# The second FFN projection by quarters with seven products

## The chip, the cores and the metric

The kernel runs on one core of a Trainium2 chip. The metric is the device time of one execution in microseconds, as a median of several runs. Three runs of the kernel before took 1961.64, 1966.53 and 1968.09 us, so its median is 1966.53 us.

Engines go by the names of the profile: PE multiplies matrices (PEld is its loading of the stationary operand), DVE and ACT work on tiles, POOL is a further engine that here does small vector work, and SP issues the transfers from device memory (HBM).

## What is computed

Two blocks run one after the other over 512 tokens of width 1024, each with two layers. The first block is left alone by the change. Each of the two layers of the second block ends in a feed-forward part (FFN), of which this is the core:

```python
def conv_ffn(x, w_up, conv_w, conv_b, w_down):
    a, g = jnp.split(x @ w_up, 2, axis=-1)
    g = lax.conv_general_dilated(g, conv_w[:, None, :].astype(g.dtype), window_strides=(1,),
                                 padding=((CONV_W - 1, 0),), dimension_numbers=('NWC', 'WIO', 'NWC'),
                                 feature_group_count=D_FF) + conv_b
    return (jax.nn.gelu(g) * a) @ w_down

    # in the layer: y = conv_ffn(...); x = layer_norm(alpha * x + y, ln_g[l, 1], ln_b[l, 1])
```

The hidden width `D_FF` is 2816, that is 22 chunks of 128. The change is about the last product, `(...) @ w_down`: 512 tokens x 2816 times 2816 x 1024.

## The kernel before

**Split numbers.** Every fp32 operand of a large product is kept as a pair (hi, lo): ACT casts the raw tile to fp32r for hi (L226 for weights), and DVE subtracts hi from the raw tile for lo (L227). One product step is then three matmuls into the same PSUM bank: hi by hi, hi by lo, lo by hi. `dsteps` (L231 to L233) has tokens as the stationary side and weights of 512 columns moving. `fsteps` (L1060 to L1062) has weights as the stationary side and 512 tokens moving.

**Weight slots.** `load_w` has SP load a raw tile (128x512, 256 KB, four buffers), takes the next of the slots in `wslots` in turn, and splits into it. Six slots are always there. `more_w` adds 7 in the FFN, so 13 in all. A slot is free again when PE has done the last matmul that reads it.

**The FFN** (`ffn`, called once a layer, the first at about 890 us, the second at about 1575 us) goes over the 22 chunks in three parts of 8, 7 and 7. Within a part, groups of at most four chunks take two passes of `fsteps`, the gate pass and the linear pass: a chunk is 8 steps of 3 matmuls, then its evacuation. `ev_g` does bias and scale on ACT (L1490), two shifted multiply-adds on DVE (L1491, L1492) and the GELU on ACT. `ev_a` multiplies by the linear half on DVE (L1497) and splits the result into `act` on ACT and DVE (L1499, L1500). Then comes the down stage of the part: for both halves of 512 output columns and the four tiles of 128 tokens, one step for each chunk of the part, and a DVE instruction that adds the bank to the running sum `z` (L1532). In the last part that is followed by the layer norm of the token tile (L1142 to L1152, with two small instructions on POOL, L281 and L282). After the first layer's FFN, the first projection of the next mixer (`start_odd`, 312 columns) is woven in between the last down steps.

**Order.** Each engine carries out its own queue in order. The queues are laid out ahead by a recording layer that interleaves the instructions by its own estimate, so they don't stand in the order of the code. Within one queue, an instruction that waits holds up all behind it.

The tile `yT` holds the mixer's output for the out projection ahead of the FFN and isn't used in it.

## Time and profile before

| | |
|---|---|
| median of three runs | 1966.53 us (1961.64 to 1968.09) |
| profiled execution, device time | 1962.12 us |
| its span, first to last instruction | 1960.3 us |
| PE busy in the span | 97% (1899.6 us, 10240 matmuls) |
| DVE, ACT, POOL busy | 60%, 40%, 10% |
| mean granted clock of PE | 0.991 of full speed |
| HBM traffic over the span | 106 GB/s |

The rows that are read from the trace stand in a section of their own below. A row gives line, engine, operation, output<-input by the program's names, and shape. In a list by time the columns are start and duration in us, and in brackets the idle time of the engine just ahead of the instruction with what ended it. Matmuls overlap: the duration of one (0.39 us) is its way through the array, and the distance between the starts of two is what it costs.

### The profile page before, as it was taken

What the parts mean: (1) busy time and instruction counts of PE and PEld (TensorE: products, weight loads), DVE (VectorE), ACT (ScalarE), POOL (GpSimd) and SP (SyncE); (2) the same over time, 40 slices, a digit from 0 to 9 for tenths busy, and PEclk for the clock granted to TensorE, in tenths of its full rate; (3) what the DMA queues carried; (4) which work ended last, traced back from release to release, by engine and by line L of the source; (5) the groups of instructions that cost most, each with busy time, mean ns of one, the idle gap of its engine ahead of it and who ended that gap; (6) DMA issues with size and microseconds to landing.
All of it is one profiled execution on the core that took longest, in us unless ns stands there. A gap on an engine that the chain in (4) does not pass through costs nothing.

```text
span 1960.3 us, 29102 instructions
## 1 busy us (share of the span) xinstructions
PE 1899.6 (97%) x10240; PEld 1540.1 (79%) x10240; DVE 1167.4 (60%) x2892; ACT 782.5 (40%) x1760; POOL 203.2 (10%) x316
## 2 busy tenths in 40 slices
PE   7999899999999999999999999999999999999998
PEld 4777687877888888768888888888778788888886
DVE  5698887475774235687434444645776774344445
ACT  2432454432553345444323333234665543233330
POOL 3011102012101000110000000101441200000001
PEclk9999999989999999999999999999999999999999
DMA  8535425135234233404322332352113042223321
GB/s 275 170 91 179 130 86 160 58 109 155 65 103 143 65 94 118 162 1 128 94 86 86 108 98 85 112 168 86 42 41 130 24 129 92 86 87 107 99 86 69
DMA packets 132872, 206.18 MB, mean 105 GB/s; under 512 B 20866, under 2 KB 57076, under 8 KB 132725
## 3 DMA queue, kind: packets, MB, share of 16 engines
q1 hardware_dynamic: 132724, 204.31, 33.9%
q8 instruction: 81, 1.33, 0.3%
q14 instruction: 67, 0.54, 0.1%
HBM read 194.62 MB, written 14.09 MB: 106 GB/s over the span
## 4 chain that ended last, share of the span: by engine, by line
PE 72%; DVE 6%; POOL 2%; DMA 1%; issue 1%; ACT 1%; POOLq 0%; DVEq 0%; ACTq 0%
PE mm L1060 11%; PE mm L1062 11%; PE mm L1061 11%; PE mm L231 9%; PE mm L233 9%; PE mm L232 8%; PE t L1095 1%; PE t L274 1%; PE o L1854 1%; PE o L1662 1%; PE mm L1924 1%; DVE w L227 1%; DVE z L1152 1%; DMA raw<-in_ffn_w_up_dram 1%; PE o L939 1%
## 5 line engine op out<-in xcount | busy, mean ns | idle before, releaser
L226 ACT CAST w<-raw 128x512 fp32r<-128x512 f32 (+4 forms) x568 | 321.8, 581 | 401.2 <-PE mm L233 172.1
L227 DVE TENSOR_TENSOR w<-raw,w 128x512 fp32r<-128x512 f32 (+4 forms) x560 | 348.4, 643 | 174.4 <-ACT w L226 171.7
L1060 PE MATMUL mm<-hT,w 128*128 128x512 f32 x920 | 367.0, 399 | 0.0
L1062 PE MATMUL mm<-hT,w 128*128 128x512 f32 x920 | 362.4, 394 | 0.0
L1061 PE MATMUL mm<-hT,w 128*128 128x512 f32 x920 | 361.6, 393 | 0.0
L231 PE MATMUL mm<-w,hT 128*128 128x512 f32 (+3 forms) x704 | 278.2, 396 | 1.2 <-ACT hT L243 1.2
L233 PE MATMUL mm<-w,hT 128*128 128x512 f32 (+3 forms) x704 | 263.2, 374 | 0.0
L232 PE MATMUL mm<-w,hT 128*128 128x512 f32 (+3 forms) x704 | 261.5, 371 | 0.5 <-DVE w L227 0.5
L1062 PEld LDWEIGHTS mm<-hT,w 128*128 128x128 f32 x920 | 172.6, 188 | 40.0 <-DVE w L227 0.8
L1060 PEld LDWEIGHTS mm<-hT,w 128*128 128x128 f32 x920 | 172.9, 188 | 39.7 <-ACT w L226 1.1
L1061 PEld LDWEIGHTS mm<-hT,w 128*128 128x128 f32 x920 | 172.9, 188 | 36.1
L231 PEld LDWEIGHTS mm<-w,hT 128*128 128x128 f32 x704 | 139.8, 199 | 30.4 <-issue 6.9
L233 PEld LDWEIGHTS mm<-w,hT 128*128 128x128 f32 x704 | 139.8, 199 | 20.7 <-issue 1.1
L232 PEld LDWEIGHTS mm<-w,hT 128*128 128x128 f32 x704 | 140.1, 199 | 16.8 <-issue 1.8
L231 PE MATMUL mm<-w,act 128*128 128x512 f32 x352 | 139.0, 395 | 0.0
L232 PE MATMUL mm<-w,act 128*128 128x512 f32 x352 | 138.3, 393 | 0.0
L233 PE MATMUL mm<-w,act 128*128 128x512 f32 x352 | 138.2, 393 | 0.0
L1532 DVE SCALAR_TENSOR_TENSOR z<-z,mm 128x512 f32<-128x512 f32 x48 | 33.0, 687 | 109.8 <-PE mm L233 109.8
L1491 DVE SCALAR_TENSOR_TENSOR g<-mm,cw,g 128x511 f32<-128x511 f32 x44 | 33.0, 749 | 100.2 <-ACT g L1490 100.2
L281 POOL TENSOR_SCALAR rp<-mv 128x1 f32<-128x1 f32 x16 | 9.8, 614 | 775.9 <-DVE mv L1146 774.9
L1090 ACT ACTIVATE E<-E,nm 128x128 f32<-128x128 f32 (+3 forms) x128 | 71.6, 560 | 45.5 <-DVE nm L1089 42.8
L1497 DVE TENSOR_TENSOR ge<-ge,mm 128x512 f32<-128x512 f32 x44 | 30.2, 686 | 83.3 <-PE mm L1062 83.3
(433 smaller groups left out, 3060.0 us busy)
## 6 DMA issues: line engine op xcount, KB each, us to landing
raw<-in_ffn_w_up_dram SPq DMA_DIRECT2D x128, 256.0 KB, 2.9
rawm<-in_w_mod_dram SPq DMA_DIRECT2D x96, 256.0 KB, 3.1
raw<-in_ffn_w_down_dram SPq DMA_DIRECT2D x88, 256.0 KB, 3.0
raw<-in_w_in_dram SPq DMA_DIRECT2D x80, 256.0 KB, 2.8
raw<-in_ev_w_in_dram SPq DMA_DIRECT2D x48, 256.0 KB, 3.1
raw<-in_ffn_w_up_dram SPq DMA_DIRECT2D x64, 192.0 KB, 2.4
raw<-in_w_out_dram SPq DMA_DIRECT2D x32, 256.0 KB, 3.0
raw<-in_w_in_dram SPq DMA_DIRECT2D x32, 128.0 KB, 3.5
```

What stands on the lines that cost most here:

```text
L226: SC.copy(hi, r)
L227: (eng or V).tensor_tensor(lo, r, hi.bitcast(F32), op=OP.subtract)
L231: PE.matmul(ps, hi, w[:, 0, w0:w0 + n], start=first, stop=False)
L232: PE.matmul(ps, hi, w[:, 1, w0:w0 + n], start=False, stop=False)
L233: PE.matmul(ps, lo, w[:, 0, w0:w0 + n], start=False, stop=last)
L1060: PE.matmul(ps, wh, hi, start=k == ks[0], stop=False)
L1061: PE.matmul(ps, wh, lo, start=False, stop=False)
L1062: PE.matmul(ps, wl, hi, start=False, stop=k == ks[-1])
L1090: SC.activation(E, E, AF.Exp, scale=scale, bias=nm, accum_out=den)
L1491: V.scalar_tensor_tensor(g0[:, 1:], ps[:, :S - 1], cw[:, 1, c:c + 1], g0[:, 1:], op0=OP.mult, op1=OP.add)
L1497: V.tensor_tensor(ge[j], ge[j], ps, op=OP.mult)
L1532: V.scalar_tensor_tensor(hs, hs, R2 if part == 0 else 1.0, ps, op0=OP.mult, op1=OP.add)
```

## The change

The parts of the FFN are now 8, 8 and 6 chunks. In the first two (`quart`), the down product is done by quarters: tokens are cut into halves of 256, output columns into halves of 512, and the chunks of the part are taken in four pairs (2p, 2p+1). The 2x2 by 2x2 product of such blocks, eight products otherwise, is done with seven of sums and differences (Strassen's scheme in Winograd's form). The last part is as before, with six chunks.

`quarters` makes the token side of a pair, after the second chunk's `ev_a`: four sums of 256 columns (DVE) and splits of three tiles of 512 and one of 256 columns (a cast on ACT and a subtraction on DVE for each). `down_quart` makes the weight side. `operand` splits four tiles `bq` into four weight slots; three of the seven sets are loaded plainly by SP, and the four others are running sums: a DMA that POOL issues adds the next quarter of the weights to the tile `bq` in place, after both halves of the split have read it. The sum `y` is used for the 1st, 3rd, 5th and 7th product, the sum `x` for the 4th and 6th, with at least one other product between two uses of one sum. `product` runs one of the seven: 4 pairs x 2 token tiles x 3 matmuls = 24 matmuls of 512 columns. Banks are added to `z` after each product's turn on them (`take`, L1537), 14 times a part.

`more_w` adds 3 slots in place of 7, so 9 in all. `g0` has three buffers in place of two, and the small tile `cwr` of the convolution weights takes one of them. Of the operand tiles of the token side, some lie in `yT`.

```diff
-        more_w(f"wf{l}", 7, fst, "left")
-        cwr = fp.tile([88, 128], F32, name="cwr")
+        more_w(f"wf{l}", 3, fst, "left")
+        cwr = fp.tile([128, S], F32, name="g0", bufs=3)[:88, :128]
...
-        for part, nch in enumerate((8, 7, 7)):
-            act = [fp.tile([128, 2, S], F32R, name="act", bufs=10) for _ in range(nch)]
+        for part, (nch, quart) in enumerate(((8, True), (8, True), (6, False))):
...
+            def quarters(p, r0, r1):
+                lh, rh = slice(0, 256), slice(256, 512)
+                k1, m, u2, v = ops[p]
+                u = fp.tile([128, S], F32, name="g0", bufs=3)
+                V.tensor_tensor(u[:, lh], r0[:, lh], r0[:, rh], op=OP.subtract)
+                V.tensor_tensor(r0[:, rh], r1[:, rh], r0[:, rh], op=OP.subtract)
+                split(m[:, 0], m[:, 1], r0)
+                split(k1[:, 0], k1[:, 1], r1)
+                V.scalar_tensor_tensor(u[:, rh], r0[:, rh], -1.0, r0[:, lh], op0=OP.mult, op1=OP.subtract)
+                split(u2[:, 0], u2[:, 1], u)
+                V.scalar_tensor_tensor(r1[:, lh], u[:, rh], -1.0, r1[:, lh], op0=OP.mult, op1=OP.subtract)
+                split(v[:, 0], v[:, 1], r1[:, lh])
...
+                def operand(name, b=None, then=None):
+                    ws = []
+                    for p in range(npair):
+                        if b:
+                            bufs[name, p] = fp.tile([128, 512], F32, name="bq", bufs=8)
+                            nc.sync.dma_start(bufs[name, p], src[b](p))
+                    for p in range(npair):
+                        wturn[0] = (wturn[0] + 1) % len(wslots)
+                        px, nx = wslots[wturn[0]]
+                        w = px.tile([128, 2, 512], F32R, tag="w", name="w", bufs=nx)
+                        split(w[:, 0], w[:, 1], bufs[name, p])
+                        ws.append(w)
+                        if then:
+                            GP.dma_start(bufs[name, p], src[then](p), accum_op=OP.add)
+                    return ws
...
+                def take(n, t, sub, ps, mul=1.0):
+                    hs = z[t][:, 512 * n:512 * n + 512]
+                    V.scalar_tensor_tensor(hs, hs, mul, ps, op0=OP.mult, op1=OP.subtract if sub else OP.add)
...
+                o1 = operand("y", (0, 0), (0, 1))
+                o2 = operand("s", (1, 0))
+                product(0, o1, X, True, False, False, lambda r, ps: take(0, r, False, ps, first))
+                o5 = operand("y", None, (1, 1))
+                product(1, o2, W, True, True, False, lambda r, ps: take(0, r, False, ps))
+                o3 = operand("x", (1, 1), (0, 1))
+                product(4, o5, Y, True, False, True, lambda r, ps: take(1, 2 + r, True, ps, first))
+                o6 = operand("y", None, (1, 0))
+                product(2, o3, Y, False, True, True, lambda r, ps: take(1, r, True, ps, first))
+                o7 = operand("x")
+                product(5, o6, X, False, False, True, lambda r, ps: take(1, r, True, ps))
+                o4 = operand("y")
+                product(6, o7, X, False, False, True, lambda r, ps: take(1, 2 + r, True, ps))
+                product(3, o4, X, False, True, True, lambda r, ps: take(0, 2 + r, False, ps, first))
```

How the queues stand now, at two places. First DVE, at the hand-over from the last linear pass of part one to its down stage, first layer. Before, the row `ge<-ge,mm` is `ev_a` and `z<-z,mm` the first use of the down product:

```order
L1497 TENSOR_TENSOR ge<-ge,mm 128x512
L227 TENSOR_TENSOR w<-raw,w 128x512
L1500 TENSOR_TENSOR act<-ge,act 128x512
L227 TENSOR_TENSOR w<-raw,w 128x512 x4
L1497 TENSOR_TENSOR ge<-ge,mm 128x512
```

And now (L1496, L1497, L1500 and L1502 are the four sums of `quarters`, L244 is the subtraction of a split, `act<-ge` the tiles m and k1, `act<-g` the tile u2, `w<-bq` weights of `operand`):

```order
L1582 TENSOR_TENSOR ge<-ge,mm 128x512
L1496 TENSOR_TENSOR g_9878<-ge 128x256
L244 TENSOR_TENSOR w<-bq,w 128x512 x7
L1582 TENSOR_TENSOR ge<-ge,mm 128x512
L244 TENSOR_TENSOR w<-bq,w 128x512
L1497 TENSOR_TENSOR ge<-ge 128x256
L244 TENSOR_TENSOR w<-bq,w 128x512
L1500 SCALAR_TENSOR_TENSOR g_9878<-ge 128x256
L244 TENSOR_TENSOR act<-ge,act 128x512 x2
L244 TENSOR_TENSOR act<-g_9878,act 128x512
L1502 SCALAR_TENSOR_TENSOR ge<-g_9878,ge 128x256
L1537 SCALAR_TENSOR_TENSOR z_8186<-z_8186,o 128x512
```

Nine weight subtractions stand ahead of the last pair's tiles, two of them (the 8th and 9th, of the third product) behind the last `ev_a`.

Second, ACT at the same place, before:

```order
L226 CAST w<-raw 128x512
L1499 CAST act<-ge 128x512
L226 CAST w<-raw 128x512 x5
L1499 CAST act<-ge 128x512
L226 CAST w<-raw 128x512 x18
L1490 ACTIVATE g_10213<-mm,cw 128x512
```

and now:

```order
L243 CAST w<-bq 128x512
L1579 ACTIVATE ge<-g_9715 128x512
L243 CAST act<-ge 128x512 x2
L243 CAST act<-g_9813 128x512
L243 CAST yT<-ge 128x256
L243 CAST w<-bq 128x512 x9
L243 CAST act<-ge 128x512 x2
L243 CAST act<-g_9878 128x512
L243 CAST w<-bq 128x512 x2
```

The casts of the last pair's tiles m and k1 (`act<-ge 128x512 x2`) stand behind nine weight casts, of which the last two read a `bq` that POOL's DMA has added to.

## Rows read from the trace of the kernel before

**Rows 1.** The page's head and busy times (us, share of the span, instructions).

```profile
span 1960.3 us, 29102 instructions
PE 1899.6 (97%) x10240; PEld 1540.1 (79%) x10240; DVE 1167.4 (60%) x2892; ACT 782.5 (40%) x1760; POOL 203.2 (10%) x316
```

**Rows 2.** Busy time by stretch, the two FFNs: length, engines, clock, DMA share, GB/s.

```profile
896.00:1262.00 366.00, 364.02 (x1667) 300.16 (x1668) 177.90 (x280) 126.16 (x214) 4.80 (x6) 1.00 0.34 102
1580.00:1952.40 372.40, 368.35 (x1688) 302.46 (x1686) 181.70 (x285) 124.03 (x210) 6.51 (x8) 1.00 0.31 97
```

**Rows 3.** The down product's first matmul of each step: ns min/median/max, first and last start.

```profile
L231 PE MATMUL mm<-w,act x352: 388/395/477, 989.3 to 1951.5; 128*128 128x512 f32 x176
```

**Rows 4.** By time, PE: first matmul of a down stage, and the first behind it.

```profile
989.26 0.40 PE L231 MATMUL mm<-w,act 128*128 128x512 f32 x1
...
1033.73 0.39 PE L1060 MATMUL mm<-hT,w 128*128 128x512 f32 x1
```

**Rows 5.** Busy time by stretch: PE, PEld, DVE, ACT, POOL; two passes, then a down stage.

```profile
944.50:989.20 44.70, 44.70 (x195) 36.29 (x194) 21.25 (x33) 17.80 (x29) 0.00 (x0) 1.00 0.32 98
989.20:1033.70 44.50, 44.50 (x193) 36.05 (x193) 16.66 (x25) 10.06 (x17) 0.00 (x0) 1.00 0.31 98
```

**Rows 6.** Groups of instructions by form: count | busy us, mean ns | idle before, releasers.

```profile
L226 ACT CAST w<-raw 128x512 fp32r<-128x512 f32 x424 | 257.2, 620 | 342.3 <-PE mm L233 158.3 <-PE mm L1062 61.0 <-DMA raw<-in_ffn_w_up_dram 41.5
L227 DVE TENSOR_TENSOR w<-raw,w 128x512 fp32r<-128x512 f32 x416 | 280.9, 695 | 132.6 <-ACT w L226 130.4
L227 DVE TENSOR_TENSOR w<-raw,w 128x256 fp32r<-128x256 f32 x48 | 19.8, 432 | 23.9 <-ACT w L226 23.5
L1532 DVE SCALAR_TENSOR_TENSOR z<-z,mm 128x512 f32<-128x512 f32 x48 | 33.0, 687 | 109.8 <-PE mm L233 109.8
L1491 DVE SCALAR_TENSOR_TENSOR g<-mm,cw,g 128x511 f32<-128x511 f32 x44 | 33.0, 749 | 100.2 <-ACT g L1490 100.2
L1497 DVE TENSOR_TENSOR ge<-ge,mm 128x512 f32<-128x512 f32 x44 | 30.2, 686 | 83.3 <-PE mm L1062 83.3
```

**Rows 7.** By time, the kernel's end: DVE's layer norm of a token tile, PE's last matmul.

```profile
1947.47 0.69 DVE L1532 SCALAR_TENSOR_TENSOR z<-z,mm 128x512 f32<-128x512 f32 x1
1948.19 0.69 DVE L1142 BATCH_NORM_STATS2 st<-z 128x6 f32<-128x512 f32 x1
1948.92 0.21 DVE L1146 BATCH_NORM_AGGREGATE mv<-st 128x2 f32<-128x12 f32 x1
1949.16 1.42 DVE L1151 SCALAR_TENSOR_TENSOR z<-z,mv,lng 128x512 f32<-128x512 f32 x2
1951.02 1.42 DVE L1152 SCALAR_TENSOR_TENSOR z<-z,rstd,lnb 128x512 f32<-128x512 f32 x2 [0.44 <-POOL rstd L282]
1951.92 0.39 PE L233 MATMUL mm<-w,act 128*128 128x512 f32 x1
1952.35 0.69 DVE L1532 SCALAR_TENSOR_TENSOR z<-z,mm 128x512 f32<-128x512 f32 x1
```

**Rows 8.** By time, PE's waits ahead of FFN passes and after the first FFN.

```profile
907.66 0.39 PE L1517 MATMUL mm<-hT,w 128*128 128x256 f32 x1 [1.98 <-ACT w L226]
1269.04 0.41 PE L232 MATMUL mm<-w,hT 128*128 128x312 f32 x1 [0.54 <-DVE w L227]
1279.21 1.29 PE L274 MATMUL t<-con,z 128*128 128x128 f32 x8 [0.36 <-DVE z L1152]
1592.70 0.39 PE L1517 MATMUL mm<-hT,w 128*128 128x256 f32 x1 [2.65 <-ACT w L226]
```

**Rows 9.** DMA issues: count, KB each, median us from issue to landing.

```profile
raw<-in_ffn_w_down_dram SPq DMA_DIRECT2D x88, 256.0 KB, 3.0
TA<-skA SPq DMA_DIRECT2D x4, 256.0 KB, 5.2
skA<-rd SPq DMA_DIRECT2D x8, 320.0 KB, 6.4
```

**Rows 10.** The page's DMA queues: packets, MB, share of 16 engines.

```profile
q1 hardware_dynamic: 132724, 204.31, 33.9%
```

More of the change, by code (lines that the diff above doesn't have):

```diff
@@ L1488, in ev_g @@
                     c = c0 + q0 + j
-                    g0 = fp.tile([128, S], F32, name="g0", bufs=2)
+                    g0 = fp.tile([128, S], F32, name="g0", bufs=3)
                     SC.activation(g0, ps, AF.Identity, scale=cw[:, 2, c:c + 1], bias=cw[:, 3, c:c + 1])
@@ L1497, in ev_a @@
                     V.tensor_tensor(ge[j], ge[j], ps, op=OP.mult)
+                    if quart:
+                        if j % 2:
+                            quarters((q0 + j) // 2, ge[j - 1], ge[j])
+                        return
                     d = act[q0 + j]
@@ L1549, in finish @@
                     save_x(t, z[t])
-            if part == 2:
-                lg = rows(1)
+            if quart:
+                down_quart()
+                c0 += nch
+                continue
+            lg = rows(1)
             w = [{k: load_w(down, 128 * (c0 + k), 512 * n, 512) for k in range(nch)} for n in range(2)]
```

33 lines of the change are left out of this document (added).

## The prediction

> **What bounds the kernel now.** I read the busy times first: PE is busy for 97% of the span, no other engine for more than 60% [rows 1]. A busy PE need not be PE at its limit, so next I read the stretches of the two FFNs: PE busy 364.0 of 366.0 us and 368.4 of 372.4 us at a granted clock of 1.00, that is 2.4 GHz, with DVE and ACT busy for under half [rows 2]. PE's only long waits there stand at the start of each FFN (1.98 and 2.65 us), with two short ones after the first [rows 8]. Within a down stage nothing is waited for: 44.50 of 44.50 us [rows 5]. So there the number of matmuls times their distance sets the time. The duration in a row (395 ns, [rows 3]) is not that distance; the starts are: the first down stage runs from 989.26 to 1033.73 us, 44.47 us for 8 chunks x 8 outputs x 3 = 192 matmuls [rows 4], **0.2316 us each**. A step of three is 0.695 us, and a pass of one chunk (8 steps) or one of the seven products (also 8 steps) 5.56 us.
>
> **The term that pays.** A part of 8 chunks took 192 matmuls and takes 7 x 24 = 168. Two parts in two layers: 4 x 24 = 96 fewer, of the same form. 96 x 0.2316 = **22.2 us**. The cut into 8, 8, 6 for 8, 7, 7 moves chunks between parts and costs no matmul. This is the ceiling, were nothing on DVE, ACT or in the DMAs late.
>
> **Load of DVE and ACT.** In a down stage there are now 28 weight subtractions at 0.695 us and 14 adds to z at 0.687 us [rows 6]: 19.5 + 9.6 = 29.1 us on DVE of 7 x 5.56 = 38.9 us, 75% where it was 16.7 of 44.5 [rows 5]. ACT has 28 casts at 0.62 us, 17.4 us. In a pass over four chunks and its gate pass (44.5 us), DVE has 16 subtractions (11.1 us), four evacuations of 0.749 x 2 + 0.686 us (8.7 us), and for each of two pairs four sums and a half split at 0.432 us (the 256-column row) and three splits at 0.695 us, 4.2 us a pair: 28.3 us, 64%. Neither engine becomes the bound by its sum. What remains is lateness at single places.
>
> **Hand-over into the down stage, four times.** Set zero at the first matmul of the first product. From the end of PE's slot to a waiting engine's start takes 0.2 us (PE's last matmul starts at 1951.92, its slot ends 0.23 us later, DVE starts at 1952.35, [rows 7]). The slot for the 7th weight that stands ahead of the last `ev_a` comes free at -0.5, its cast ends at 0.12 and its subtraction at 0.85. Then DVE's queue goes: `ev_a` to 1.54, the third product's first weight to 2.23, a sum to 2.66, its second weight to 3.35 (slot free at 1.6, cast done at 2.2), a sum to 3.78, the low half of m to 4.47. PE needs m of the last pair at step 6 of the first product, 4.17, and the low half for its third matmul, 4.63. So the margin is **0.16 us**: about nothing, and I charge 0.4 us each, **1.6 us**. Later in the stage each set is split about one product ahead of its use, since its slots come free when the product two ahead ends; banks and adds to z likewise have half a product or more.
>
> **The adding DMAs.** Their work is new: the trace has no DMA that POOL issues (all data goes by one queue, [rows 10]) and none that adds. The tightest one is the second `y` tile: split by -3.36, and its sum is read at 1.6, at the latest at 2.2 if m is not to be late. So issue to landing may take **5.6 us**. A plain load of that size takes 3.0 us; another source of the same size shows 5.2, and the slowest median shown is 6.4 [rows 9]. I take it near 3.0, as the nearest in size and source, with room for the second read: no wait. At 6.4 it costs 0.8 us x 4 = 3.4 us. It can't be below zero, since nothing waits for DMA there today. The later sums have 7 us or more from split to use. The Trainium skill ("DMA: Bandwidth & Descriptors", Anatomy of one DMA — SWDGE path) gives for a DMA issued by GpSimd 2.0 us plus bytes by 436 GB/s, an estimate of 2.6 us for 256 KB, with no price for an add; by it there is no wait either. No row here shows it. Queued behind them on POOL is only the layer norm at the FFN's end. SP now loads 12 tiles a part where it loaded 16, and POOL adds 16; the DMA engines are 33.9% busy [rows 10]. In SP's queue, the loads for the next part's sums wait for tiles that the 6th and 7th product free, about 28 us into the stage, and raw loads for the next part's fifth and later weights wait behind them. Those are used from 3 us after the stage's end at 38.9: some 10 us of cover for loads of 3.0 us, so nothing; without the cover it is one load, 3 us a part.
>
> **Nine slots in place of thirteen.** Between two passes, weight k of the next pass can only be split when step k of the last chunk is done, and is needed one pass (5.56 us) later. Release, cast and subtraction take 0.2 + 0.62 + 0.695 = 1.5 us. But DVE must do 8 subtractions (5.6 us) and two gate evacuations (3.0 us), or a pair's 4.2 us with two `ev_a`, in about 11 us. Walking the queue as it now stands, the last weights come some 0.7 us (gate to linear) and 1.0 us (linear to gate) ahead of need. There are 9 such hand-overs a layer; I charge 0.1 us each, **1.8 us**, with bounds 0 and 0.6 us each.
>
> **The two ends.** In the last down stage a token tile takes PE 6 chunks x 3 x 0.2316 = 4.17 us, before 7 x 3 x 0.2316 = 4.86. DVE's chain for a tile runs from 1947.47 to 1952.44 with hardly a gap, 4.9 us [rows 7]: so far it just kept up. Now it falls back 0.73 us a tile, three times: **2.2 us** at the kernel's end, nothing hides it. After the first FFN the same chain feeds transposes that other matmuls cover; waits of 0.54 and 0.36 us stand there [rows 8], and with the weights of `start_odd` now waiting for slots I add **0.5 us** (0 to 2).
>
> **The starts.** The waits of 1.98 and 2.65 us name weight casts that stand ahead of the last token casts in ACT's queue. Now five of the first weights are split earlier. I count **1 us** back (bounds: 4.6 us back, 3 us lost).
>
> **The sum.** 22.2 - 1.6 - 1.8 - 2.2 - 0.5 + 1.0 = **17 us**. Against the profiled execution (1962.1 us) that is 1945. This execution is near the fastest of the three runs; the mean of the four times is 1964.6 us. From there: **1947.5 us**.
>
> **Rivals.**
> 1. *The starts free up and the walk holds:* 22.2 - 2.2 + 4 = 24 us, 1938 to 1941. For it: the margins above are positive. Against: the waits at the start may be of the transfers themselves.
> 2. *Nine slots bind:* at 0.5 to 0.6 us for each of 18 hand-overs, 9 to 11 us in place of 1.8: gain 8 to 10 us, 1955 to 1957. For it: margins under 1 us on a chain of three engines, and DVE's queue is in order. Against: DVE is below 75%, and a late weight makes up time in the next pass.
> 3. *Adding DMAs land late.* Each us past 5.6 holds ACT's queue at the 9th cast, behind it m, and with it PE, in each of four stages. At 7 to 9 us from issue to landing it costs 6 to 14 us: 1953 to 1961. **From 9.9 us on the gain of 17 is gone, and at 12 us the kernel is slower: 1973 us.** For it: four such DMAs follow each other from one engine in 3 us. Against: no row of this size is above 5.2 us. The Trainium skill ("SBUF — State Buffer", SBUF: two separate sides) warns that a DMA issued by GpSimd starves while DVE runs a 2-port operation (3100 for 620 ns there); by its section Who interferes with whom, tensor_tensor, which the subtractions here are, has no such mode. No row here shows either.
>
> **How the numbers follow.** The forecast (1942 to 1953) gets 0.64, rival 1 0.08, rival 2 0.10, rival 3 up to 1961 us 0.09, and beyond that 0.09. The range for 8 in 10 takes the forecast and rivals 1 and 2: 1938 to 1958. A measurement of this kernel can tell about 0.3%, 5.9 us. Faster by more are the forecast, rivals 1 and 2 and two thirds of the partly late DMAs, 0.88, of which I take 0.06 off to within 0.3%, since late DMAs and short slots can add up: 0.82. Within 0.3% then are 0.03 + 0.01 + 0.06 = 0.10, slower 0.08.
>
> **What would show it.** PE with 10144 matmuls, 96 fewer than 10240 [rows 1]. Down stages of some 39 us. A wait of PE for DVE's m (L244) or ACT's cast within the first product speaks for the hand-over term; if ACT's `w<-bq` rows there show idle time that a DMA ended, it is rival 3, and the DMA rows give its landing. PE waits for L227 at passes' starts speak for rival 2. At the end, DVE's last chain starts 2 us or more after PE's last matmul. Wrong would be all of this if the distance of matmuls in the new stage isn't 0.23 us.

## The result and the profile after

The changed kernel took a median of 1939.75 us in four runs (1935.72 to 1946.16) where the kernel before took 1965.76 (1961.64 to 1968.09). The ratio is 0.9882, 95% interval 0.9843 to 0.992: some 23 us faster. The prediction was 1947.5 us with a range from 1938 to 1958 us, so the direction and the range held, while the gain is larger than the 17 us of the forecast. The median lies in the band of rival 1 (1938 to 1941 us), not in that of the forecast (1942 to 1953 us); a later repeat of the same kernel took 1942.69 us, so the time alone does not tell the two apart, and the stages below have to.

The profiled execution of the changed kernel took 1936.26 us. First the page's head, the busy times and the queue that is new (packets, MB, share of 16 engines), to be read against [rows 1] and [rows 10]:

```profile
span 1934.5 us, 29305 instructions
PE 1874.2 (97%) x10144; PEld 1518.6 (79%) x10144; DVE 1251.6 (65%) x3060; ACT 828.1 (43%) x1840; POOL 260.1 (13%) x380
q0 software_dynamic: 9216, 16.78, 5.2%
```

PE has its 96 matmuls less, and DVE is at 65%. Next, busy time by stretch. The columns are the stretch, its length, busy time of PE, PEld, DVE, ACT and POOL with counts, granted clock, DMA share and GB/s. The stretches are the first FFN's half stage (its first gate pass, in halves of 256 tokens), the four Strassen stages, the second FFN's half stage (fourth row), and the last down stage to the kernel's end:

```profile
893.58:918.49 24.91, 24.32 (x203) 23.92 (x201) 12.80 (x21) 9.23 (x15) 1.68 (x2) 1.00 0.59 191
985.00:1024.30 39.30, 39.30 (x170) 31.44 (x168) 30.20 (x50) 19.15 (x33) 10.55 (x12) 1.00 0.91 209
1112.42:1151.28 38.86, 38.86 (x170) 31.53 (x169) 30.34 (x50) 19.14 (x33) 10.57 (x12) 1.00 0.76 158
1563.49:1591.71 28.22, 25.90 (x211) 24.90 (x209) 17.29 (x29) 11.26 (x19) 1.45 (x2) 1.00 0.56 189
1658.30:1697.41 39.11, 39.04 (x170) 31.45 (x168) 30.33 (x50) 19.11 (x33) 10.55 (x12) 1.00 0.91 211
1785.57:1824.56 38.99, 38.99 (x170) 31.52 (x168) 30.53 (x50) 19.19 (x33) 10.61 (x12) 1.00 0.77 158
1890.65:1934.50 43.85, 33.68 (x145) 26.83 (x143) 28.67 (x45) 4.11 (x8) 6.75 (x8) 0.92 0.23 79
```

A Strassen stage takes 38.9 to 39.3 us, and 7 x 5.56 is 38.9. DVE is busy for 30.2 to 30.5 us in it, where the prediction summed 29.1. So the term that pays came in full, and nearly nothing was lost inside the stages. The half stages tell where the surplus is: 24.91 and 28.22 us. The kernel before needed 28.42 and 29.01 us for them.

The prediction's tightest place is the hand-over into the first Strassen stage, whose first matmul is at 985.00. By time, POOL's adding DMAs (L1525) and ACT's casts (L243), with start, duration and in brackets the idle time ahead and what ended it:

```profile
982.02 2.64 POOL L1525 DMA_DIRECT2D bq<-in_ffn_w_down_dram  x3 [13.35 <-DVE w L244]
...
986.65 0.62 ACT L243 CAST w<-bq 128x512 fp32r<-128x512 f32 x1 [0.78 <-PE o L1549]
987.48 1.14 ACT L243 CAST act<-ge 128x512 fp32r<-128x512 f32 x2 [0.21 <-DVE ge L1497]
988.53 0.62 ACT L243 CAST act<-g 128x512 fp32r<-128x512 f32 x1
989.35 0.62 ACT L243 CAST w<-bq 128x512 fp32r<-128x512 f32 x1 [0.20 <-DMA bq<-in_ffn_w_down_dram]
991.53 0.62 ACT L243 CAST w<-bq 128x512 fp32r<-128x512 f32 x1 [1.56 <-DMA bq<-in_ffn_w_down_dram]
```

The sum of the second tile is cast at 986.65, 1.65 us behind the first matmul as the walk had it, and what it waited for is PE's slot, not its DMA. The third and fourth tiles do wait for their DMAs, but ACT has cast the last pair's token tiles (`act<-ge`) ahead of them, so PE feels nothing. DVE, at the same place:

```profile
985.83 0.68 DVE L1582 TENSOR_TENSOR ge<-ge,mm 128x512 f32<-128x512 f32 x1
986.43 0.68 DVE L244 TENSOR_TENSOR w<-bq,w 128x512 fp32r<-128x512 f32 x1
...
988.31 1.29 DVE L244 TENSOR_TENSOR act<-ge,act 128x512 fp32r<-128x512 f32 x2
```

An instruction starts 0.08 us before the one ahead of it has ended (986.43 against 986.51), which the prediction's walk, a sum of durations, did not allow for. So the low half of the last pair's m is done 3.99 us into the stage and not at 4.47, and the margin of 0.16 us was really 0.64. All adding DMAs of this execution, duration on POOL in ns and the time from issue to landing:

```profile
L1525 POOL DMA_DIRECT2D bq<-in_ffn_w_down_dram x64: 853/1080/2547, 967.6 to 1803.5; - x64
DMA to landing us min/median/max: 3.9/7.7/10.8
```

The prediction's bounds were 3.0 and 6.4 us, so a burst lands far later than they allowed. Of the three issued from 982.02 on, the landings come after 3.9, 6.5 and 8.0 us, that is at 985.9, 989.3 and 991.4. In all bursts, one landing follows another after 0.9 to 3.6 us, 1.7 us in the median. The tight one is the first of its burst and lands after 3.9 us, within the 5.6 us that the prediction gave it.

The end answers [rows 7]. PE's last matmul, and DVE's use of its bank:

```profile
1923.94 0.40 PE L233 MATMUL mm<-w,act 128*128 128x512 f32 x1
...
1926.44 0.68 DVE L1621 SCALAR_TENSOR_TENSOR z<-z,mm 128x512 f32<-128x512 f32 x1
```

2.50 us lie between them where it was 0.43: DVE has fallen back by 2.1 us.

### The profile page after: what moved, and what is told of

It is laid out like the page before. It is cut to its first block, busy times and chain, and to the rows that moved or that the text cites. A ratio compares the mean times of both kernels' runs of the same rounds, so it can differ in the third digit from the quotient of the medians.

```text
span 1934.5 us, 29305 instructions
## 1 busy us (share of the span) xinstructions
PE 1874.2 (97%) x10144; PEld 1518.6 (79%) x10144; DVE 1251.6 (65%) x3060; ACT 828.1 (43%) x1840; POOL 260.1 (13%) x380
## 4 chain that ended last, share of the span: by engine, by line
PE 65%; DVE 7%; issue 6%; POOL 3%; DMA 2%; ACT 1%; POOLq 0%; DVEq 0%; SPq 0%; ACTq 0%
PE mm L1060 10%; PE mm L1062 10%; PE mm L1061 9%; PE mm L231 6%; PE mm L233 6%; PE mm L232 6%; PE t L1095 1%; PE o L1547 1%; PE o L1549 1%; PE o L1548 1%; DMA bq<-in_ffn_w_down_dram 1%; PE mm L1547 1%; PE mm L1549 1%; PE mm L1548 1%; PE t L274 1%
## 5 line engine op out<-in xcount | busy, mean ns | idle before, releaser
L227 DVE TENSOR_TENSOR w<-raw,w 128x512 fp32r<-128x512 f32 (+4 forms) x496 | 307.5, 638 | 140.1 <-ACT w L226 138.4
L226 ACT CAST w<-raw 128x512 fp32r<-128x512 f32 (+4 forms) x504 | 284.5, 575 | 239.8 <-PE mm L233 55.9
L1525 POOL DMA_DIRECT2D bq<-in_ffn_w_down_dram x64 | 56.6, 1280 | 413.0 <-DVE w L244 401.7
L243 ACT CAST w<-bq 128x512 fp32r<-128x512 f32 x112 | 69.0, 621 | 65.1 <-DMA bq<-in_ffn_w_down_dram 20.2
L244 DVE TENSOR_TENSOR w<-bq,w 128x512 fp32r<-128x512 f32 x112 | 75.5, 689 | 15.4 <-ACT w L243 14.8
L1575 ACT ACTIVATE g<-mm,cw 128x512 f32<-128x512 f32 x44 | 34.2, 777 | 79.6 <-PE mm L1062 63.1
L1085 DVE COPY pT<-t 128x512 f32<-128x512 f32 (+3 forms) x84 | 43.0, 512 | 37.8 <-PE t L1280 23.3
```

What stands on the lines that cost most here:

```text
L226: SC.copy(hi, r)
L227: (eng or V).tensor_tensor(lo, r, hi.bitcast(F32), op=OP.subtract)
L243: SC.copy(hi, ps)
L244: V.tensor_tensor(lo, ps, hi.bitcast(F32), op=OP.subtract)
L1525: GP.dma_start(bufs[name, p], src[then](p), accum_op=OP.add)
```

## The experiments

Stage lengths below are from the start of a stage's first matmul to the start of the next stage's first. In single profiled executions they agree to a few hundredths where nothing waits, while whole spans of one kernel differ by 5 us and more, mostly ahead of the FFNs. So the stages decide what the total times cannot. Each run has one profiled execution, so a stage in which something waits is known from that one alone.

### What shortened the starts

In the kernel before, SP's queue at the first FFN's start stands as follows: three gate weights (the fifth to the seventh), then the two rows of the layer norm (`lng`, `lnb`, 512 KB each, needed 300 us later), then the eighth gate weight.

```profile
895.87 2.20 SPq L213 DMA_DIRECT2D raw<-in_ffn_w_up_dram  x3
899.07 0.33 SPq L286 DMA_DIRECT2D lng<-in_ln_g_dram  x1
900.39 0.33 SPq L286 DMA_DIRECT2D lnb<-in_ln_b_dram  x1
901.00 24.27 SPq L213 DMA_DIRECT2D raw<-in_ffn_w_up_dram  x14
```

ACT's cast that PE waits for at 907.66 [rows 8] waited itself, and for a load:

```profile
906.99 0.62 ACT L226 CAST w<-raw 128x512 fp32r<-128x512 f32 x1 [4.59 <-DMA raw<-in_ffn_w_up_dram]
```

In the changed kernel all eight gate weights stand ahead of these rows in the first FFN. In the second, loads of the down product's weights (`bq`) and of `lng` stand between the gate weights. The theory is that this order sets the start. The rivals are fewer slots, or ACT's order, by themselves.

**The kernel before with the two rows loaded late:**

```diff
-        def rows(i):
+        def rows(i, dep=None):
             lg = [zp.tile([128, D], F32, name=n, bufs=1) for n in ("lng", "lnb")]
+            for g in lg if dep is not None else ():
+                SC.copy(g[:, 0:1], dep)
...
             if part == 2:
-                lg = rows(1)
+                lg = rows(1, act[0][:, 0, 0:1].bitcast(F32))
```

ACT copies one column of the last part's first chunk into each row's tile, and the load of the row has to wait for that copy.

> The kernel before, 13 slots, with one thing moved: the two layer norm rows of the FFN (lng, lnb) are loaded only after the first chunk of the last part is split (a copy of one column into each tile makes them wait), so that in both FFNs no load stands between the gate weights in SP's queue. Theory (SP's order sets the starts): half stages fall from 28.4 and 29.0 us to about 25 us each, some 7 us in all, with the waits of 1.98 and 2.65 us gone. Rival (what shortened the start is the earlier split of weights, that is fewer slots or ACT's order): both stay within 0.5 us of 28.4 and 29.0.

Measured: 1959.59 us, ratio 0.998 (0.9954 to 1.0006), so that the total alone would not show the gain. Both half stages, of the kernel before and then of this one:

```profile
894.36:922.78 28.42, 26.14 (x202) 25.41 (x201) 17.98 (x29) 12.65 (x22) 1.45 (x2) 0.94 0.54 158
1579.23:1608.24 29.01, 25.05 (x207) 24.20 (x206) 19.44 (x32) 14.82 (x26) 1.45 (x2) 1.00 0.51 155
```

```profile
892.04:916.92 24.88, 24.59 (x203) 23.91 (x201) 18.08 (x29) 12.76 (x22) 1.45 (x2) 1.00 0.46 139
1573.29:1599.56 26.27, 24.96 (x208) 24.24 (x206) 19.60 (x32) 15.00 (x26) 1.45 (x2) 1.00 0.43 131
```

With 13 slots and nothing else changed, the first half stage falls to 24.88 us, the length that the changed kernel has (24.91), and the second to 26.27 us. So SP's order is shown to be enough. Of the 3.5 us in the first, PE's idle time gives 2.0 (2.28 to 0.29 us); the rest goes with the granted clock, 0.94 before and 1.00 now, which fell behind the wait. That fall need not come each time: the kernel with parts of 8, 8 and 6, below, starts its first FFN in the same order, waits 2.55 us at this place with the clock at 1.00, and takes 27.50 us.

**The kernel before with nine slots:**

```diff
-        more_w(f"wf{l}", 7, fst, "left")
+        more_w(f"wf{l}", 3, fst, "left")
```

> The kernel before with 9 weight slots in place of 13, nothing else. Its queues show a side effect: in the first FFN SP now issues ten weight loads ahead of the two layer norm rows (lng, lnb) where it issued seven, so all eight gate weights come before them; in the second FFN it is six in both kernels. Theory (order in SP's queue sets the starts): half stage of the first FFN 28.4 to about 25 us, that of the second stays at 29.0, and slots cost nothing elsewhere (passes of 5.5 us a chunk): some 3.4 us faster than before. Prediction's own term: slots cost 0.1 us at 18 places, 1.8 us. Rival 2 of the prediction (nine slots bind): 9 to 11 us slower, with PE waiting for L227 at the starts of passes. If both starts shorten alike, the slots and not SP's order give the gain.

Measured: 1956.97 us, ratio 0.995 (0.9926 to 0.9974). The first half stage and the passes of parts two and three in the first FFN, and then those passes in the kernel before:

```profile
892.18:916.68 24.50, 24.40 (x201) 24.14 (x202) 13.67 (x23) 9.98 (x17) 1.45 (x2) 1.00 0.39 120
1027.79:1104.93 77.14, 77.14 (x337) 63.03 (x336) 36.80 (x60) 30.24 (x53) 0.00 (x0) 1.00 0.31 94
1143.94:1221.04 77.10, 77.10 (x337) 63.03 (x336) 36.25 (x58) 30.41 (x52) 0.00 (x0) 1.00 0.30 93
```

```profile
1033.73:1111.24 77.51, 77.51 (x338) 63.03 (x336) 36.79 (x59) 30.19 (x53) 0.00 (x0) 1.00 0.31 94
1150.09:1227.62 77.53, 77.53 (x337) 63.04 (x336) 36.27 (x59) 30.40 (x52) 0.00 (x0) 1.00 0.30 93
```

Here the slots changed SP's order only in the first FFN, and there the half stage fell by 3.9 us; in the second it still went from 29.01 to 27.60, which SP's order doesn't explain, so that fewer slots seem to have a hand of 1.4 us in it (three executions of the changed kernel have 27.95 to 28.53 us there). In parts two and three nine slots cost nothing: PE is busy without a gap, and the passes are even 0.4 us shorter, since matmuls stand 0.2296 us apart (77.14 / 336) and not 0.2307. From the half stage to the first linear pass they do cost something:

```profile
921.17 0.50 PE L1060 MATMUL mm<-hT,w 128*128 128x512 f32 x1 [0.19 <-ACT w L226]
```

ACT's cast ahead of it waited for the load of its weight. PE waits 0.19 us here and 0.45 us in the second FFN, and the passes of part one take 66.57 and 66.94 us, where the same 288 matmuls at 0.2295 would take 66.1. The kernel before has no such wait there. That is 0.5 and 0.8 us at one of nine hand-overs a layer; the others held. Rival 2, with 0.5 us at each, falls.

### The tail and the count of matmuls

**The kernel before with parts of 8, 8 and 6** (`enumerate((8, 7, 7))` to `enumerate((8, 8, 6))`):

> The kernel before with parts of 8, 8 and 6 chunks in place of 8, 7, 7, nothing else; 10240 matmuls as before. Tail term of the prediction: DVE's chain for a token tile (4.9 us) falls behind PE's 4.17 us three times, so the end comes 2.2 us later and after the first FFN 0 to 0.5 us are lost; the span grows by 2.2 to 2.7 us. Half stages stay at 28.4 and 29.0 us if parts have no hand in the starts. Rival: DVE has slack enough from the first half of the last stage and the tail costs nothing.

Measured: 1966.5 us, ratio 1.0012 (0.9994 to 1.0031). The last down stage and the tail take 43.34 us where they took 47.03, 3.69 less; the 24 matmuls that went elsewhere are 5.56. So the tail costs 1.87 us. After the first FFN the same reckoning gives 52.44 for 57.88 us, a loss of 0.12. The half stages are 27.50 and 28.81 us; the 0.9 us less in the first comes with a clock that did not fall (1.00 for 0.94), so parts have little to do with the starts.

**The changed kernel with seven products in the first part only** (the second part's `True` to `False`; the layer norm's rows are loaded in the last part alone, as before):

> The changed kernel with seven products in the first part only; the second part's down product is as in the kernel before, with 8 chunks. 48 matmuls more than the changed kernel. Theory (the gain is the number of matmuls alone, at 0.2316 us): second down stages of 44.5 us where the changed kernel has 38.9 and 39.0, so 11.1 us more than the changed kernel, some 1951 us. Rival (hand-overs into the Strassen stages or the adding DMAs cost something hidden, or later stages give back): the difference is below 10 or above 12 us.

Measured: 1952.87 us, ratio 0.9928 (0.9902 to 0.9953). The second part's down stages:

```profile
1115.07:1159.75 44.68, 44.68 (x194) 36.02 (x192) 16.70 (x25) 10.16 (x17) 0.00 (x0) 1.00 0.30 99
1793.67:1838.35 44.68, 44.68 (x194) 36.01 (x192) 16.75 (x25) 10.32 (x17) 0.00 (x0) 1.00 0.31 99
```

With eight products they take 44.68 us each, with seven 38.86 and 38.99: 11.5 us for 48 matmuls, where 11.1 were expected. The gain is the number of matmuls, and nothing gives it back later.

### What the adding DMAs cost

**The changed kernel once more:**

> The changed kernel as it is, on the same chip as the three others, for comparison: a ratio of about 0.988 to the kernel before; down stages of 38.9 to 39.3 us, half stages of 24.9 and 28.2 us, 43.85 us from the start of the last down stage to the end.

Measured: 1942.69 us, ratio 0.9885 (0.9859 to 0.9911). Second and fourth Strassen stage are as before (38.85 and 38.99), but the first took 41.18 us and the third 39.50. In the first, landings reached 12.3 us, and this is what came of it in the sixth product, ahead of its second token tile:

```profile
1022.35 0.62 ACT L243 CAST w<-bq 128x512 fp32r<-128x512 f32 x1 [1.37 <-DMA bq<-in_ffn_w_down_dram]
...
1023.00 0.69 DVE L244 TENSOR_TENSOR w<-bq,w 128x512 fp32r<-128x512 f32 x1 [1.29 <-ACT w L243]
1023.61 0.68 DVE L1537 SCALAR_TENSOR_TENSOR z<-z,o 128x512 f32<-128x512 f32 x1
...
1024.35 0.50 PE L1547 MATMUL o<-w,act 128*128 128x512 f32 x1 [1.83 <-DVE z L1537]
```

A late sum holds ACT's cast, the cast holds DVE's subtraction, and behind that, in DVE's queue, stands the addition to `z` that must read the bank before PE adds to it again. The lateness reaches PE by a bank, not by a weight. Late sums holding ACT's queue are rival 3's mechanism, but the way to PE is another one, and it opens five products later than the prediction placed it.

**Adds behind the whole set:** POOL was to issue the four adds of a set only after its four splits.

```diff
                         ws.append(w)
-                        if then:
-                            GP.dma_start(bufs[name, p], src[then](p), accum_op=OP.add)
+                    for p in range(npair if then else 0):
+                        GP.dma_start(bufs[name, p], src[then](p), accum_op=OP.add)
```

> The changed kernel with one thing moved: POOL issues the four adding DMAs of a set after all four splits of the set, not one after each split. The order on all other engines is unchanged. In the trace of the changed kernel the first split of y ends at 981.7 us and the first add is issued at 982.0 and lands after 3.9 to 4.7 us, where ACT wants the sum at 986.65, so about 0.7 us are to spare. Here the first add can't be issued before about 984.0. Theory (the prediction's threshold: 5.6 us from split to landing, then PE waits us for us): the sum lands at 987.9 to 988.7, ACT's 9th cast and behind it m of the last pair come 1.3 to 2.0 us later, and PE waits 0.7 to 1.5 us in the first product of each of the four stages, 3 to 6 us in all. Rival (there is a cushion that the walk did not see): first product without waits above 0.3 us, time as the changed kernel's.

Measured: 1940.7 us, ratio 0.9878 (0.9851 to 0.9904), with the second tile's add still issued 2.98 us ahead of the stage (the expectation takes it for the first tile's, which goes out 17 us ahead). The recording layer laid the queues of DVE, ACT, POOL and SP out as they had been, so nothing was moved: it is a repeat. Its first stage took 40.35 us, with a wait of 1.02 us at the same bank.

**POOL held up ahead of a set's first add:**

> The changed kernel with POOL held up ahead of the first adding DMA of each of the four Strassen stages: one POOL addition of 128x512 (1.3 us) that reads the split tile, and one more adding DMA of 256 KB into an idle buffer. The result is the reference's, and the queues of PE, DVE and ACT are as in the changed kernel. In the changed kernel the first add is issued 3.0 us ahead of the stage's first matmul and lands 0.9 us behind it, ACT casts the sum at 1.65, and by the prediction's walk PE begins to wait if it lands after 2.2. Here it should land some 3.3 us later, at about 4.2. Theory (the walk and its threshold hold): PE waits about 2 us (1.5 to 2.5) in the first product of each stage, and all sums come later, so the four stages take 8 to 10 us more in all, some 1949 us. Rival (DVE's and ACT's queues have more room than the walk says): stages longer by less than 1 us each.

Measured: 1940.55 us, ratio 0.9869 (0.9835 to 0.9903); stages of 39.54, 38.85, 38.78 and 38.99 us. Nothing was held up that matters: the first tile's slot is free early, its add goes out 17 us ahead of the stage, and the prediction's threshold is about the second tile. Another near repeat. Over six executions with the kernel's 16 adds in their places (the changed kernel, these three and the two variants at the end), the four stages together lie 0.2 to 2.9 us above 4 x 38.9, about 1 on average. The waits stand only in the first part's stages, at that one bank.

**Plain loads by POOL in place of adds** (`accum_op` left out, so that the weight sums, a part of the computation, are missing):

> The changed kernel with the 64 adding DMAs turned into plain loads of the same tiles, still issued by POOL (the add is left out, so the weight sums are not those of the reference). It measures what the add itself costs against the way by POOL. If the add is the price: landings fall from 3.9/7.7/10.8 us (min, median, max) towards the 3.0 us of a plain load that SP issues. If the way by POOL is the price: landings stay within 1 us of the changed kernel's. In both cases theory says that PE does not wait for these DMAs, so the time stays within 0.3% of the changed kernel's.

Measured: 1943.34 us, ratio 0.9887 (0.986 to 0.9914).

```profile
L1525 POOL DMA_DIRECT2D bq<-in_ffn_w_down_dram x64: 536/536/779, 980.4 to 1815.2; - x64
DMA to landing us min/median/max: 2.8/3.7/5.7
```

So the add doubles the landing: median 7.7 for 3.7 us, where SP's loads have 3.0 [rows 9]. The four stages are 39.09, 38.86, 38.77 and 38.98 us, 0.1 us above 4 x 38.9, with no wait at that bank. It fits that the loss comes from the adds' lateness; but two of the six executions with adds lie only 0.2 and 0.3 us above, so one execution does not settle it. The Trainium skill ("DMA: Bandwidth & Descriptors", Anatomy of one DMA — SWDGE path) has a fit that gives an estimate of 2.6 us for 256 KB; the fastest plain one (2.8 us) comes near it, the median of the plain ones and the adding ones don't. The Trainium skill's warning of a DMA that starves beside a 2-port operation of DVE ("SBUF — State Buffer", SBUF: two separate sides) can't be the reason for the slow adds: the plain ones ran beside the same DVE work.

**The second tile's add held up:** one POOL addition that reads the split tile, and one more adding DMA, both into an idle buffer (`dum`), ahead of the add that the threshold is about.

```diff
                         ws.append(w)
+                        if then and p == 1 and b == (0, 0):
+                            GP.tensor_tensor(dum, bufs[name, p], w[:, 1].bitcast(F32), op=OP.add)
+                            GP.dma_start(dum, src[then](p), accum_op=OP.add)
                         if then:
```

> As the kernel that held POOL up ahead of the first add of a stage, but at the second tile, which is the one that the prediction's threshold is about (the first tile's slot was free so early that its add is issued 17 us ahead of the stage, so that holding it up changed nothing). Here, behind the split of the second tile, POOL does one addition of 128x512 and one adding DMA into an idle buffer before the add of the second tile. In the changed kernel that add is issued at 982.02, 2.98 us ahead of the stage's first matmul, and lands after 3.9 us, 0.9 us behind it; ACT casts the sum at 1.65, and by the walk PE waits if it lands after 2.2. Here it is issued some 2.3 us later, as the second of a burst, which takes about 6.5 us to land: 5.3 to 5.8 us behind the first matmul. Theory (5.6 us from split to landing, then us for us): PE waits 3 to 3.6 us in the first product of each stage, for DVE's or ACT's part of the token tiles, 12 to 15 us in all, some 1953 us. Rival (a cushion that the walk does not see): less than 1 us a stage.

Measured: 1967.83 us, ratio 1.0019 (0.9998 to 1.0041): the whole gain is gone. Stages of 46.56, 45.60, 44.98 and 45.24 us, 26 us more than in the changed kernel. The first of them begins at 983.93. By time, POOL, ACT and PE, and then three stretches of it (the granted clock is the third number from the end):

```profile
980.73 1.75 POOL L1526 TENSOR_TENSOR g<-bq,w 128x512 f32<-128x512 f32 x1 [13.01 <-DVE w L244]
982.78 0.88 POOL L1527 DMA_DIRECT2D g<-in_ffn_w_down_dram  x1 [0.31 <-POOL g L1526]
983.37 2.96 POOL L1529 DMA_DIRECT2D bq<-in_ffn_w_down_dram  x3
...
991.69 0.62 ACT L243 CAST w<-bq 128x512 fp32r<-128x512 f32 x1 [6.90 <-DMA bq<-in_ffn_w_down_dram]
...
992.88 0.80 PE L1551 MATMUL o<-w,act 128*128 128x512 f32 x1 [4.59 <-ACT act L243]
```

```profile
983.93:992.50 8.57, 4.36 (x19) 3.18 (x17) 3.20 (x7) 1.62 (x4) 3.25 (x4) 0.94 0.91 191
992.90:998.40 5.50, 5.50 (x13) 3.96 (x13) 4.96 (x11) 3.03 (x6) 0.86 (x1) 0.51 0.83 161
998.40:1030.49 32.09, 32.09 (x139) 25.88 (x138) 22.63 (x35) 14.18 (x23) 8.82 (x10) 1.00 0.82 189
```

The add lands 8.2 us after its issue, 10.9 us after the split, and is cast 7.76 us behind the first matmul. PE waits, as the walk said, for ACT's cast of the last pair's token tile, which stands behind that cast. Its wait is 4.8 us (8.95 us into the stage in place of 4.17): counted us for us, the cast could have come at 3.0 without harm, where the prediction put the point at 2.2. So the mechanism holds, and the threshold within 0.8 us. But PE loses more than it waits: behind the wait the granted clock is 0.51, that is 1.2 GHz, for 5.5 us, with matmuls 0.43 us apart. These 13 matmuls cost 2.5 us on top, and 4.8 + 2.5 is what the stage lost, 7.3 us. The Trainium skill ("TensorE: Matmul & The Clock Gate", Wait — 56ns, not 53.3ns?) has 426.7 ns between matmuls of 512 columns at the low clock, which the trace agrees with, and 215.7 at the high one, where a stage without waits shows some 231 (38.86 us for 168).

**One more adding DMA in every set:**

> The changed kernel with one more adding DMA in each of the four sets of a stage (20 in place of 16), into an idle buffer, behind the first add of a set; the result is the reference's. In the traces so far the adds of a burst land some 2 us apart, so that 16 of them are 32 us of a stage of 38.9 us, and 20 would be 40 us. Theory (the queue of adding DMAs is near its limit, and its lateness reaches PE by ACT's casts and DVE's in-order queue, as with the one wait of 1.8 us in a repeat of the changed kernel): the adds become the bound, each stage 2 to 8 us longer, 8 to 30 us in all. Rival (bursts are only queueing, with room between them): stages longer by less than 1 us each, since a set has about one product of time to spare.

Measured: 1965.3 us, ratio 0.999 (0.9969 to 1.0011); stages of 43.83, 45.63, 46.82 and 43.08 us, 23 us more. The extra DMA stands ahead of the first add of a set, not behind it as the expectation has it, and the run doesn't show what it was made for. POOL's queue in the first stage:

```profile
986.07 1.58 POOL L1527 DMA_DIRECT2D g<-in_ffn_w_down_dram  x1
995.99 0.86 POOL L1527 DMA_DIRECT2D g<-in_ffn_w_down_dram  x1 [8.34 <-DMA g<-in_ffn_w_down_dram]
996.53 2.10 POOL L1529 DMA_DIRECT2D bq<-in_ffn_w_down_dram  x2
```

The extra DMA writes one buffer, so the second waits 8.34 us for the first, and the kernel's own adds stand behind it. It shows again that lateness there reaches PE, by the bank (PE waits 2.52 us for `z`, L1541). Whether 20 adds are too many for the queue stays open.

### Two variants

**Loads late, and the last stage tile by tile:** the first eight `bq` tiles wait for the first split pair of chunks and the layer norm's rows for the first split chunk of the last part; the second layer's last down stage does both column halves of a token tile in turn, with four of its weights in idle operand tiles.

> The changed kernel with two more edits. The layer norm rows and the first eight weight tiles of the down product are loaded only after the first pair of chunks is split, so that all gate weights stand ahead of them in SP's queue; and in the second layer the last down stage goes tile by tile (both column halves of a token tile before the next tile), with four of its weights in idle operand tiles, so that the layer norm's chain has 8.3 us a tile and not 4.2. Theory: half stage of the second FFN 28.2 to 25 or 26 us, first FFN 24.9 as it is; the end after the last down stage's start 43.85 to about 41.5 us; in all 4 to 5 us less than the changed kernel. Rival: the weights of the last stage come late as twelve are now wanted in its first 8.3 us (8.3 us of subtractions on DVE), and eat up what the tail gives.

Measured: 1948.18 us, ratio 0.9909 (0.9893 to 0.9925): by the median 5.5 us more than the repeat of the changed kernel beside it, though the intervals overlap. The second half stage fell to 26.84 us, but the passes behind each grew from 66.5 to 67.9 us. SP's queue there:

```profile
940.09 1.32 SPq L1521 DMA_DIRECT2D bq<-in_ffn_w_down_dram  x3
943.32 2.41 SPq L213 DMA_DIRECT2D raw<-in_ffn_w_up_dram  x4
```

Weights of the next pass (`raw`) stand behind loads that wait for a split pair. The last stage also starts with a wait of 1.95 us for its weights, behind which the granted clock is 0.81 over the stage's first 9.2 us, and takes 44.68 us to the end, not less than 43.8: the rival came true. The tail itself did what it was made for: DVE takes the bank of PE's last matmul 0.42 us behind it (1937.02 and 1937.44), where the changed kernel has 2.50.

**Loads after the first gate chunk only:**

```diff
+                            if part == 0 and name != "x":
+                                SC.copy(bufs[name, p][:, 0:1], tok[0])
                             nc.sync.dma_start(bufs[name, p], src[b](p))
```

`tok` is a small tile with a column of the first `ge`; the layer norm's rows wait for it likewise.

> The changed kernel with the first eight weight tiles of the down product and the layer norm rows loaded only after the first gate chunk of the FFN is evacuated (a copy of one column makes them wait), so that SP's queue has nothing between the gate weights. Theory: half stage of the second FFN from 28.2 to 26 or 27 us, that of the first as it is, 24.9; nothing else moves, 1 to 2 us less than the changed kernel, below what the time can tell. Rival (seen in the kernel that loaded them still later): weights of the next pass stand behind the waiting loads in SP's queue, and the passes up to the down stage grow from 66.5 us by a microsecond or more each.

Measured: 1935.45 us, ratio 0.9849 (0.9823 to 0.9876). It beats the kernel before, and by the medians the changed kernel too, but the intervals overlap. The second half stage is 27.01 us, 1.2 less, as expected. The larger part of what its profile gained has another cause, which is open: passes of parts two and three of 87.08 and 65.33 us where the changed kernel has 88.12 and 66.10, in both FFNs, with PE busy all through and the clock at 1.00. Their matmuls stand 0.2268 us apart in place of 0.2295. (It is the only kernel here with one more small tile, `tok`; whether that has to do with it was not tried.) The rival came true in part: the passes of part one, with as many matmuls as those of part three (65.33 us), take 66.96 and 66.43, and PE waits 1.34 us in the first of them for a weight.

## Why the prediction was right, and where not

Profile to profile the span fell by 25.8 us. Step by step, each first as forecast and then as it was, in us of gain:

| term | forecast | found | from |
|---|---|---|---|
| 96 matmuls | 22.2 | 22.2 | count, and stages of 38.9 to 39.3 |
| Strassen stages beyond that | -1.6 | -0.6 | 156.26 less 4 x 38.9 |
| slots, 18 hand-overs | -1.8 | +1.7 | passes of parts two and three, 155.0 to 154.2 and 155.2 to 154.3; part one as before |
| tail | -2.2 | -2.4 | 43.84 for 47.03, less 24 matmuls; 1.87 alone |
| after the first FFN | -0.5 | -0.5 | 52.83 for 57.88, less 24 matmuls |
| starts | +1.0 | +4.3 | half stages, 3.5 and 0.8 |
| outside the FFNs | 0 | +1.2 | 0.8 ahead of the first, 0.4 between them; one kernel's own executions differ by more |

The found gains sum to 25.9 us. The direction, the main term and the tail came true by their mechanism. Nearly all other terms erred to the same side, by some 9 us together, and the time came out 1.75 us above the lower end of the range; that it is still inside is in part luck, since neither the narrower spacing of matmuls nor SP's order was in the prediction.

- **The count of matmuls and their distance** held, and with them the argument from a stretch in which PE waits for nothing [rows 4, 5].
- **The tail** was right in mechanism and size. DVE's chain of 4.9 us against 4.17 for a tile was all that was needed.
- **The starts** are, with the slots, the term that was mis-sized most: 1 us taken, 4.3 found, inside the bound of 4.6. Some 1.7 us of the 4.3 (28.42 us at a mean clock of 0.94) is the clock's fall in the one profiled execution of the kernel before. The prediction read the waits of [rows 8] as casts in ACT's queue and noted that they might be transfers. They were, by their order: what ACT waited for was a load behind two rows that nobody needed yet. ACT's and SP's rows at that place would have shown it. The step that failed is that only what was named as the releaser (ACT) was read, and not what ended ACT's own wait.
- **The slots** were charged at 18 places; the margins of 0.7 and 1.0 us, walked by hand, held at 16 of them. At the other two, from the half stage to the first linear pass, PE waits 0.12 and 0.10 us for a cast whose weight was loaded late, and the passes of part one take 66.5 and 66.6 us where the same matmuls take 66.1 in part three: some 0.9 us in all, in place of 1.8. That passes of parts two and three became shorter, by 0.8 and 0.9 us a layer, was outside the bounds; it has to do with the spacing of matmuls and not with lateness. The wider spacing with 13 slots is seen in three kernels, and its cause is open.
- **The hand-over** has no loss at the place where 0.16 us of margin was found; the margin was 0.64. Where a stage loses, PE waits for a bank late in the stage, behind sums that landed late, 0.2 to 2.9 us an execution. The charge of 1.6 us is near that, but its reason was not the right one.
- **The adding DMAs** were mis-priced: near 3.0 us, at most 6.4, was the forecast, and 3.9 to 10.8 us is what the trace shows. The nearest row in size and source was one without an add. It did no harm as the one tight DMA is the first of a burst and landed after 3.9 to 4.7 us in the four stages; that was luck, since the prediction didn't ask where in a burst it stands. The threshold of 5.6 us was right to 0.8 us, and 10.9 us from split to landing took 26 us, as rival 3 said of the region beyond 9.9 us; with the clock's fall it is dearer than a microsecond for each.

Rival 1 is what happened, for its first reason, but the starts were freed by SP's order, which it didn't name. Rival 2 is refuted by the kernel with nine slots alone. Rival 3 is real: the second tile's sum lands 0.9 us into the stage, and from 3.0 us on PE pays.

## What to carry to other kernels

Where PE waits for nothing in a stretch, matmuls saved there are time saved, at their distance; the losses then come from single places, and one walk through the queues at the tightest of them finds its margin to a microsecond. A wait that names an engine should be followed one step further, to what that engine waited for, and a load that nobody needs soon should not stand in a queue ahead of one that is awaited. Moving it back too far, behind a wait, blocks the queue for all that follow.

## What the runs showed of the hardware

- An adding DMA of 256 KB from POOL with no earlier one on its way took 3.9 to 4.7 us to land (8 cases), and the median of all 64, most of them in bursts, is 7.7 us, one landing 1.7 us behind the other in the median. Plain ones on the same way took 2.8 to 4.2 us (12 cases) and 3.7 in the median.
- A wait of 4.6 us of PE brought the granted clock to 0.51 for the next 5.5 us, and the 1.98 us of [rows 8] left its half stage at a mean of 0.94. A wait of 1.83 us in a Strassen stage was followed by no slow matmuls, and neither were the 2.65 us of [rows 8], 2.55 us with parts of 8, 8 and 6, and 2.52 us with one more add in every set. So the length of the wait alone doesn't tell whether the clock falls. A stall of PE can cost half as much again as it lasts.
- Matmuls of the same queue, with PE never idle and the clock at 1.00, stood 0.2268, 0.2295 or 0.2307 us apart in the first FFN of different kernels. What sets this was not tried.
